# A mixture-of-experts loop with the picking matmuls ahead of the scatter group and other PSUM banks for scatter and gather

## The chip, the core and the metric

The kernel runs on one core of one Trainium2 chip. The metric is device time of one execution in microseconds (us), lower is better. The core's engines run side by side, each with a queue of its own that it works off strictly in order: TensorE (PE; its weight loads are shown as PEld), VectorE (DVE), ScalarE (ACT), GpSimd (POOL), and SyncE (SP), which here issues the DMAs. A matmul writes to PSUM, which this kernel uses as eight tiles of 128 partitions x 512 float32 values; such a tile is called a bank below. DVE and ACT read a bank, and only then may a later matmul overwrite it.

## What is computed

One decoder layer on 512 tokens of width 1024: an attention part, then a hierarchical mixture of experts with 32 experts and two chosen per token. The change lies wholly in the second part, which is, cut to its core:

```python
for e in range(N_EXPERTS):
    h = jax.nn.silu(t @ w_gate[e]) * (t @ w_up[e])
    y = y + combine[:, e:e + 1] * (h @ w_down[e]).astype(jnp.float32)
```

Here `combine` holds the gates of the two chosen experts of each token and zero elsewhere. A 1024 x 512 gate matrix, a 1024 x 512 up matrix and a 512 x 1024 down matrix belong to each expert, all float32.

## The kernel before

The kernel does not run every expert over every token. It handles the 32 experts as 16 pairs (`NP = 16`, counted by `q`). For each pair it gathers up to 64 tokens of each expert into 128 rows, computes with these rows alone, and adds the result back to the residual `hx` (512 x 1024, held in SBUF). Gathering and adding back are matmuls with one-hot matrices. The steps of one pair:

- `pick_a` (L766) and `pick_h` build the one-hot matrix `ohh` (DVE) and a bfloat16 copy `ohb` (ACT).
- `pick_g` (L803) is twelve very small matmuls (L809, 4 columns each) that pick the gate, the token number and the norm factor of each gathered row into bank `pm`. Two small DVE copies (L811, L812) move them to `idf`.
- `x_rows` (L834), called twice, gathers the rows of the normed input: 32 matmuls of 128 x 128 in each call (L839), then one DVE multiply (L843) that empties the bank into `xT`. The first call (`g` = 0) uses bank `pm`, the second bank `po`.
- `mm_in` (L941) is the gate product (`u` = 0) and the up product (`u` = 1); the second ends with a DVE multiply into `sg` (L958). `h_t` (L962) transposes that result through a bank `pt`, and `mm_down` (L971) is the down product, in two halves of 512 columns. `ev_down` (L987) moves each half to SBUF as a pair `yh`, `yl`.
- `comb` (L1084) adds one half to the residual for one block of 128 tokens `i`: two matmuls (L1092, L1093) into a bank, then one DVE addition to `hx` (L1094). `combs` (L1145) calls it for `i` = 0, 1, 2, 3; this is the scatter group. The banks are `pm`, `po`, `pt`, `pt` in this order.
- `over_prep` (L996), once, at pair 1, counts the tokens that do not fit into 64 rows: four matmuls (L999) into `po`, four DVE instructions that read it (L1001, L1003), then a chain on POOL. `over_loop` at the end of the program treats those tokens; in the profiled execution it made no round.

The order is written out by hand in the loop at L1149 and no scheduler changes it. In iteration `q` the products of pair `q` run, and the rows of pair `q + 1` are gathered. After the up product of pair `q` the order is: the scatter group for the second half of pair `q - 1`, (`over_prep` if `q` = 1), `pick_g(q + 1)`, `x_rows(q + 1, 0)`, `h_t(q)`, `x_rows(q + 1, 1)`, the down product and the scatter group for the first half of pair `q`.

Bank names stand for pools: there is one `pm`, one `po`, two `pt`, two `pjt` (down product) and two `ps_s` (gate and up product). Weights come by DMA into a ring of 21 units of 1 MB (plus one spare); `load` (L619) issues the next unit when the matmuls that read the old content have been passed, in the order gate, up, down of each pair. The down weights of the last two pairs come last, in smaller pieces (L631). At the end `finish` (L1098) runs the down product of these two pairs in column pieces (L1105), adds and stores.

Of the kernel before, what the change touches and what calls it, by code (L numbers as in the profile page):

```python
# [10 lines left out]
F32 = mybir.dt.float32  # L11
# [28 lines left out]
    g=[5, 10, 7, 12, 6, 1, 1],  # L40
# [544 lines left out]
def moe(ctx, tc, A, out, G):  # L585
    nc = tc.nc
    v, act, pool, pe = nc.vector, nc.scalar, nc.gpsimd, nc.tensor
    hx, ident, mhalf, bcast, spool, pt_tile, warm, colv, colx, rb = (
        G[k] for k in ("hx", "ident", "mhalf", "bcast", "spool", "pt_tile", "warm", "colv", "colx", "rb"))
    pj, psS, psT, psO, psM, split_wo, OPS = (G[k] for k in ("pj", "psS", "psT", "psO", "psM", "split_wo", "OPS"))  # L590
    out = out[0]
    NS = 21
    NP = 16
# [20 lines left out]
    def rows(q, u, e, k):  # L614
        if u == 2:
            return place(AT[q, u], k)[:, e]
        return place(AT[q, u], k // 2)[:, e, 512 * (k % 2):512 * (k % 2) + 512]

    def load(half=None):  # L619
        m, c = divmod(state["n"], 4)  # L620
        state["n"] += half != 0
        if m < 3 * NP - 2:
            d, w = place(m, c), src(m, c)
            if half is not None:
                d, w = (x[:, :, 512 * half:512 * half + 512] for x in (d, w))
            nc.sync.dma_start(d, w)
        elif m < 3 * NP and c == 3:
            cut = CUT[MO[m][0]]
            for lo, hi in zip(cut, cut[1:]):
                for k in range(4):  # L630
                    nc.sync.dma_start(place(m, k)[:, :, lo:hi], src(m, k)[:, :, lo:hi])  # L631
# [62 lines left out]
    def tmp(n, *shape, dt=F32, tag=None):  # L694
        return me.tile([128] + list(shape), dt, name=n, tag=tag or n)
# [77 lines left out]
    def pick_h(q):  # L773
        OHB[q] = me.tile([128, 4, 128], BF16, name="ohb")
        if q:
            act.activation(OHB[q], OHH[q], AF.Copy)
        else:
            act.activation(OHB[q][:, :2], OHH[q][:, :2], AF.Copy)
            act.activation(OHB[q][:, 2:], OHN[q][:, 2:], AF.Copy)
# [7 lines left out]
    def half(i, c):  # L787
        return H[i // 2][:, c, i % 2]
# [14 lines left out]
    def pick_g(q):  # L803
        p = psM.tile([128, 512], F32, name="pm")
        for i in range(4):
            for j in range(3):
                c = g3[:, j, i, 0:1]
                c = bass.AP(tensor=c.tensor, offset=c.offset, ap=[list(c.ap[0]), [2 + 2 * q, 2], [1, 2]])
                pe.matmul(p[:, 0:4], OHB[q][:, i, :], c, start=(i == 0 and j == 0), stop=(i == 3 and j == 2))  # L809
        ID[q] = me.tile([128, 3], F32, name="idf", bufs=3)  # L810
        v.tensor_copy(ID[q], p[:, 0:3])  # L811
        v.tensor_copy(ID[q][64:128, 2:3], p[64:128, 3:4])  # L812
# [19 lines left out]
                v.tensor_scalar(x, t, g, None, op0=OP.mult)  # L832

    def x_rows(q, g):  # L834
        p = (psO.tile([128, 4, 128], F32, name="po") if g else psM.tile([128, 4, 128], F32, name="pm"))
        for k in range(4):
            for i in range(4):
                for c in range(2):
                    pe.matmul(p[:, k, :], half(i, c)[:, 4 * g + k, :], OHH[q][:, i, :],  # L839
                              start=(i == 0 and c == 0), stop=(i == 3 and c == 1))  # L840
        if g == 0:
            XT[q] = G["m2_"].tile([128, 8, 128], F32, name="xT")
        v.tensor_mul(XT[q][:, 4 * g:4 * g + 4, :], p, colg[:, 4 * g:4 * g + 4].unsqueeze(2).to_broadcast([128, 4, 128]))  # L843
# [97 lines left out]
    def mm_in(q, u, fill=()):  # L941
        p = psS.tile([128, 512], F32, name="ps_s")
        for k in range(8):
            for e in range(2):
                pe.matmul(p[64 * e:64 * e + 64, :], XT[q][:, k, 64 * e:64 * e + 64], rows(q, u, e, k),  # L945
                          start=(k == 0), stop=(k == 7))
            if q == 0 and 8 * u + k < PRM["qk"]:
                if k // 2 != 2 or u:
                    load(k % 2)
            elif k % 2 and (q or u or k != 5):  # L950
                load()
            for j in range(k * len(fill) // 8, (k + 1) * len(fill) // 8):
                fill[j]()
        if u == 0:
            GT[q] = me.tile([128, 512], F32, name="sg")
            act.activation(GT[q], p, AF.Silu, scale=1.0 if q else ID[q][:, 0:1])
        elif q:
            v.tensor_mul(GT[q], GT[q], p)  # L958
        else:
            v.scalar_tensor_tensor(GT[q], p, ID[q][:, 0:1], GT[q], op0=OP.mult, op1=OP.mult)  # L960

    def h_t(q):  # L962
        t = pt_tile()
        for k in range(4):
            pe.transpose(t[:, k, :], GT[q].rearrange("p (c k) -> p k c", k=4)[:, k], ident)  # L965
        HT[q] = me.tile([128, 4, 128], F32, name="hTt", tag="ohn" if q == NP - 2 else "sg")
        act.activation(HT[q], t, AF.Copy)  # L967
# [16 lines left out]
    def y_pair(q):  # L984
        return [me.tile([128, 512], F32R, name=f"y{c}", tag=f"y{c}") for c in "hl"]

    def ev_down(q, n):  # L987
        yh, yl = YH[q, n] = y_pair(q)
        p = DN.pop((q, n))
        g = ID[q][:, 2:3]  # L990
        act.activation(yh, p, AF.Copy, scale=g)  # L991
        v.scalar_tensor_tensor(yl, p, g, yh, op0=OP.mult, op1=OP.subtract)  # L992
# [3 lines left out]
    def over_prep():  # L996
        p = psO.tile([128, 512], F32, name="po")
        for i in range(4):
            pe.matmul(p[:, :32], one, mb[:, i, :], start=(i == 0), stop=(i == 3))  # L999
        te, ca, cb = tmp("te", 32), tmp("ca", 32), tmp("cb", 32)  # L1000
        v.tensor_scalar(te, p[:, :32], 64.0, None, op0=OP.is_gt)  # L1001
        for j in range(1, 4):
            v.scalar_tensor_tensor(te, p[:, :32], 64.0 + 128.0 * j, te, op0=OP.is_gt, op1=OP.add)  # L1003
        cur, nxt = te, ca
        for d in (1, 2, 4, 8, 16):
            pool.tensor_copy(nxt[:, :d], cur[:, :d])
            pool.tensor_add(nxt[:, d:], cur[:, d:], cur[:, :32 - d])
            cur, nxt = nxt, (cb if nxt is ca else ca)
        pool.tensor_sub(te, cur, te)
        c2 = me.tile([128, 4, 32], F32, name="c2", tag="L")  # L1010
        pool.tensor_scalar(nxt, te, 128.0, -64.0, op0=OP.mult, op1=OP.add)
        pool.tensor_add(c2, code, nxt.unsqueeze(1).to_broadcast([128, 4, 32]))
        nt = me.tile([128, 1], I32, name="nt")
        pool.tensor_copy(nt, cur[:, 31:32])
        gi = tmp("gi", 1)
        pool.memset(gi, 0.0)
        OV.update(lo=te, hi=cur, scr=nxt, c2=c2, gi=gi, nt=nt)
# [66 lines left out]
    def comb(q, n, i, store=False):  # L1084
        yh, yl = YH[q, n]
        ns = slice(512 * n, 512 * n + 512)
        if i < 2 or store:
            p = psO.tile([128, 512], F32, name="po") if i % 2 else psM.tile([128, 512], F32, name="pm")
        else:
            p = pt_tile().rearrange("p a b -> p (a b)")  # L1090
        oh = OH[q][:, 128 * i:128 * i + 128]
        pe.matmul(p, oh, yh, start=True, stop=False)  # L1092
        pe.matmul(p, oh, yl, start=False, stop=True)  # L1093
        v.tensor_add(hx[:, i, ns], hx[:, i, ns], p)  # L1094
        if store:
            nc.sync.dma_start(out[128 * i:128 * i + 128, ns], hx[:, i, ns])
# [48 lines left out]
    def combs(q, n):  # L1145
        for i in range(4):
            comb(q, n, i)

    for q in range(NP):  # L1149
        fill = []  # L1150
        if q == 0:
            fill = [lambda: None, lambda: pick_g(0), lambda: pick_h(1)]
        elif q == 1:
            fill = [lambda: None, lambda: combs(0, 0), lambda: ev_down(0, 1)]
        if q < NP - 1:
            pick_a(q + 1)
            if q:
                pick_h(q + 1)
        mm_in(q, 0, fill)
        if q == 0:  # L1160
            split_h(2)
            split_h(3)
        mm_in(q, 1)
        if 0 < q < NP - 1:
            combs(q - 1, 1)
        if q == 1:
            over_prep()
        if q < NP - 1:
            pick_g(q + 1)
            x_rows(q + 1, 0)  # L1170
        h_t(q)
        if q < NP - 1:
            x_rows(q + 1, 1)
        oh_s(q)
        if q == 0:
            mm_down(q, (0, 1))
            ev_down(q, 0)
        elif q < NP - 2:
            mm_down(q, (0,))
            ev_down(q, 0)  # L1180
            mm_down(q, (1,))
            combs(q, 0)
            ev_down(q, 1)
    finish()
    over_loop()

# [59 lines left out]
```

## Time and profile before

| what | value |
|---|---|
| time, median of 3 runs | 800.59 us (799.62 to 801.36) |
| the profiled execution: its own time | 800.3 us |
| its span, first to last instruction | 798.5 us |
| mean granted TensorE clock | 0.994 of full speed |
| PE busy | 760.6 us, 95% of the span |
| DVE busy | 386.5 us, 48% |
| ACT busy | 198.0 us, 25% |
| POOL busy | 121.8 us, 15% |

The profile is one execution. Its times count from the first instruction; the time of the execution is 1.8 us longer than the span. A row of the trace names source line, engine, operation, the tile written and the tiles read, and in brackets for how long the engine had been idle before it and what ended that. Idle time of an engine off the path that ends last costs nothing.

### The profile page before, as it was taken

The numbers are of one execution on the slowest core, as the hardware profiler recorded it, in microseconds if no ns is written. First come the engines' busy times: TensorE is split into PE (matmuls) and PEld (weight loads), VectorE is DVE, ScalarE is ACT, GpSimd is POOL, SyncE is SP. The second block draws the span as 40 slices with busy tenths as digits, with TensorE's granted clock in tenths as the row PEclk, the third lists the DMA queues.
The fourth block names the chain that finished last, engine by engine and source line by source line (L and its number), as shares of the span: only waits on it lengthen the run. The fifth ranks groups of instructions, "written<-read, shape, count | busy, mean of one in ns | idle before, by whom it ended". The sixth has DMA issues, their size and how long they took to land.

```text
span 798.5 us, 12313 instructions
## 1 busy us (share of the span) xinstructions
PE 760.6 (95%) x4848; PEld 473.0 (59%) x4848; DVE 386.5 (48%) x924; ACT 198.0 (25%) x426; POOL 121.8 (15%) x213
## 2 busy tenths in 40 slices
PE   8989999999999999999999999999999999999996
PEld 8868877888967884344443443443543543544455
DVE  5787887777877364333333322422522423333234
ACT  6534445444552434100100100101101001001011
POOL 2767551432312120010000000000000000000000
PEclk9999999999999999999999999999999999999999
DMA  8522022244576888999999999999999999999603
GB/s 327 174 80 70 11 87 85 95 139 153 211 275 212 317 309 297 385 345 412 405 409 408 407 408 409 409 408 408 408 409 409 409 409 408 407 409 364 209 1 108
DMA packets 78140, 231.68 MB, mean 290 GB/s; under 512 B 5113, under 2 KB 20857, under 8 KB 78081
## 3 DMA queue, kind: packets, MB, share of 16 engines
q1 hardware_dynamic: 78080, 230.88, 76.1%
q8 instruction: 39, 0.64, 0.3%
q14 instruction: 21, 0.16, 0.1%
HBM read 228.75 MB, written 2.11 MB: 289 GB/s over the span
## 4 chain that ended last, share of the span: by engine, by line
PE 75%; DVE 15%; DMA 3%; ACT 3%; issue 1%; POOL 1%; SPq 1%; DVEq 0%; ACTq 0%
PE ps_s L945 26%; PE pjt L977 12%; DVE hx L1094 4%; PE pm L839 4%; PE po L839 3%; PE pjt L226 3%; DMA wr<-in_wq_dram 3%; PE pjt L228 3%; PE pjt L227 3%; PE po L389 2%; PE pjt L1105 2%; PE pjt L448 2%; PE ps_s L356 2%; PE pjt L449 2%; PE pjt L450 2%; PE pt L382 2%
## 5 line engine op out<-in xcount | busy, mean ns | idle before, releaser
L958 DVE TENSOR_TENSOR sg<-sg,ps_s 128x512 f32<-128x512 f32 x15 | 10.3, 687 | 170.6 <-PE ps_s L945 170.6
L967 ACT ACTIVATE hTt<-pt 128x512 f32<-128x512 f32 x16 | 9.6, 597 | 186.2 <-PE pt L965 186.2
L991 ACT ACTIVATE yh<-pjt,idf 128x512 fp32r<-128x512 f32 x28 | 19.2, 687 | 134.0 <-PE pjt L977 70.3
L364 ACT ACTIVATE z<-z,sm 128x128 f32<-128x128 f32 (+3 forms) x64 | 35.5, 555 | 42.9 <-DVE sm L362 42.7
L251 POOL TENSOR_TENSOR ss<-ss,mhalf 128x4 f32<-128x4 f32 x32 | 34.8, 1088 | 60.2 <-DVE ss L250 55.9
L839 PEld LDWEIGHTS <-ha 128*128 128x128 f16 x480 | 32.0, 98 | 19.2 <-DVE idf L812 19.1
L992 DVE SCALAR_TENSOR_TENSOR yl<-pjt,idf,yh 128x512 fp32r<-128x512 f32 x28 | 20.9, 747 | 42.0 <-ACT yh L991 42.0
L839 PE MATMUL pm<-ohh,ha 128*128 128x128 f16 x240 | 23.3, 220 | 17.7 <-DVE idf L812 17.7
L227 PE MATMUL pjt<-wsa,xh 128*128 128x384 f32 (+1 forms) x112 | 37.9, 339 | 0.2 <-DVE wsa L149 0.2
L1094 DVE TENSOR_TENSOR hx<-hx,pm 128x512 f32<-128x512 f32 x28 | 19.1, 683 | 37.8 <-PE pm L1093 37.8
L1094 DVE TENSOR_TENSOR hx<-hx,pt 128x512 f32<-128x512 f32 x56 | 35.7, 679 | 0.0
L839 PEld LDWEIGHTS <-hb 128*128 128x128 f16 x480 | 31.8, 98 | 0.0
L226 PE MATMUL pjt<-wsa,xh 128*128 128x384 f32 (+1 forms) x80 | 29.2, 365 | 0.8 <-ACT wsa L148 0.8
L383 DVE COPY PT<-pt 128x128 f32<-128x128 f32 (+3 forms) x64 | 28.2, 481 | 1.8 <-PE pt L382 1.5
L945 PE MATMUL ps_s<-slotr,xT 128*64 128x512 f32 x128 | 28.9, 594 | 0.0
L356 PE MATMUL ps_s<-qks 64*128 64x128 f32 (+3 forms) x192 | 25.5, 356 | 3.4 <-DVE sm L362 2.0
L228 PE MATMUL pjt<-wsa,xl 128*128 128x384 f32 (+1 forms) x80 | 27.1, 339 | 0.0
L227 PE MATMUL pjt<-wsu,xh 128*128 128x384 f32 (+1 forms) x76 | 25.8, 340 | 0.5 <-DVE wsu L149 0.5
L382 PE MATMUL pt<-ident,z 128*128 128x128 f32 x160 | 23.5, 277 | 3.0 <-DVE PT L383 1.7
L226 PE MATMUL pjt<-wsu,xh 128*128 128x384 f32 (+1 forms) x72 | 26.3, 365 | 0.0
L945 PE MATMUL ps_s<-slotxh,xT 128*64 128x512 f32 x112 | 25.4, 595 | 0.0
L945 PE MATMUL ps_s<-slot,xT 128*64 128x512 f32 x112 | 25.3, 594 | 0.0
(426 smaller groups left out, 1737.3 us busy)
## 6 DMA issues: line engine op xcount, KB each, us to landing
wr<-in_wq_dram SPq DMA_DIRECT2D x28, 384.0 KB, 3.9
slotr<-in_w_up_dram SPq DMA_DIRECT2D x8, 1024.0 KB, 8.0
slotr<-in_w_gate_dram SPq DMA_DIRECT2D x8, 1024.0 KB, 13.1
slot<-in_w_gate_dram SPq DMA_DIRECT2D x8, 1024.0 KB, 13.5
slotwr<-in_w_up_dram SPq DMA_DIRECT2D x8, 1024.0 KB, 15.8
slotr<-in_w_down_dram SPq DMA_DIRECT2D x8, 1024.0 KB, 11.7
slotxh<-in_w_up_dram SPq DMA_DIRECT2D x7, 1024.0 KB, 10.2
slotmhl<-in_w_gate_dram SPq DMA_DIRECT2D x7, 1024.0 KB, 14.4
```

Of the source, the lines that this page charges most:

```text
L226: pe.matmul(ps[:, :n], xh[:, k, t], wh, start=(k == 0), stop=False)
L227: pe.matmul(ps[:, :n], xh[:, k, t], wl, start=False, stop=False)
L228: pe.matmul(ps[:, :n], xl[:, k, t], wh, start=False, stop=(k == 7))
L251: pool.tensor_tensor(ss[:, 4:8], ss[:, 0:4], mhalf[:, 0:4], op=OP.pow)
L356: pe.matmul(pss[h][:, :n], q[d, t], k[d, :n], start=(k is kh and q is qh), stop=(q is ql))
L364: act.activation(z[:, :n], z[:, :n], AF.Exp, bias=nm, scale=-1.0, accum_out=l)
L382: pe.transpose(t[:, j, :], z[:, 128 * j:128 * j + 128], ident)
L383: v.tensor_copy(PT[p][h][:, :i + 1, 128 * i:128 * i + 128], t[:, :i + 1, :])
L839: pe.matmul(p[:, k, :], half(i, c)[:, 4 * g + k, :], OHH[q][:, i, :], start=(i == 0 and c == 0), stop=(i == 3 and c == 1))
L945: pe.matmul(p[64 * e:64 * e + 64, :], XT[q][:, k, 64 * e:64 * e + 64], rows(q, u, e, k), start=(k == 0), stop=(k == 7))
L977: pe.matmul(DN[q, n][64 * e:64 * e + 64, :], HT[q][:, k, 64 * e:64 * e + 64], rows(q, 2, e, k)[:, 512 * n:512 * n + 512], start=(k == 0), ...
L1094: v.tensor_add(hx[:, i, ns], hx[:, i, ns], p)
```

## The change

Three things change, and no arithmetic does. First, in the loop at L1149 `pick_g(q + 1)` is called right after the up product, ahead of the scatter group. Second, `over_prep` of pair 1 moves from there to the end of that iteration. Third, banks are handed out in another order: `x_rows` uses `po` for its first call and `pm` for its second, and the scatter group uses `po`, `pt`, `pt`, `pm`. (`comb` with `store`, which `over_loop` alone uses, alternates between `po` and `pm` as before, with the two swapped.)

```diff
     def x_rows(q, g):
-        p = (psO.tile([128, 4, 128], F32, name="po") if g else psM.tile([128, 4, 128], F32, name="pm"))
+        p = (psM.tile([128, 4, 128], F32, name="pm") if g else psO.tile([128, 4, 128], F32, name="po"))
...
     def comb(q, n, i, store=False):
-        if i < 2 or store:
-            p = psO.tile([128, 512], F32, name="po") if i % 2 else psM.tile([128, 512], F32, name="pm")
+        if i in (1, 2) and not store:
+            p = pt_tile().rearrange("p a b -> p (a b)")
         else:
-            p = pt_tile().rearrange("p a b -> p (a b)")
+            p = psO.tile([128, 512], F32, name="po") if i in (0, 2) else psM.tile([128, 512], F32, name="pm")
...
         mm_in(q, 1)
+        if q < NP - 1:
+            pick_g(q + 1)
         if 0 < q < NP - 1:
             combs(q - 1, 1)
-        if q == 1:
-            over_prep()
         if q < NP - 1:
-            pick_g(q + 1)
             x_rows(q + 1, 0)
...
             ev_down(q, 1)
+            if q == 1:
+                over_prep()
```

On TensorE, behind an up product in the middle of the loop, the kernel before has (`yh` and `yl` are the evicted down product, `ohs` the one-hot matrix that scatters, `g` and `ohb` the operands of the picking, `ha` a part of the normed input):

```order
L945 MATMUL ps_s<-slotqkb,xT 64x512 x4
L1092 MATMUL pm<-yh,ohs 128x512
L1093 MATMUL pm<-yl,ohs 128x512
L1092 MATMUL po<-yh,ohs 128x512
L1093 MATMUL po<-yl,ohs 128x512
...
L809 LDWEIGHTS ohb
L809 MATMUL pm<-g_2976,ohb 128x4
...
L839 LDWEIGHTS ha
L839 MATMUL pm<-ohh,ha 128x128
```

and the changed kernel:

```order
L945 MATMUL ps_s<-slotqkb,xT 64x512 x4
L809 LDWEIGHTS ohb
L809 MATMUL pm<-g_2976,ohb 128x4
...
L1092 MATMUL po<-yh,ohs 128x512
L1093 MATMUL po<-yl,ohs 128x512
...
L1092 MATMUL pm<-yh,ohs 128x512
L1093 MATMUL pm<-yl,ohs 128x512
L839 LDWEIGHTS ha
L839 MATMUL po<-ohh,ha 128x128
```

The picking moved ahead of the eight scatter matmuls, the last scatter bank is now the one that the picking wrote, and the gather's first bank is the one that the scatter group wrote first.

On VectorE the same place reads before:

```order
L958 TENSOR_TENSOR sg<-sg,ps_s 128x512
L1094 TENSOR_TENSOR hx<-hx,pm 128x512
L1094 TENSOR_TENSOR hx<-hx,po 128x512
L1094 TENSOR_TENSOR hx<-hx,pt 128x512 x2
L811 COPY idf<-pm 128x3
L812 COPY idf<-pm 64x1
L843 TENSOR_TENSOR xT<-pm,colg 128x512
L843 TENSOR_TENSOR xT<-po,colg 128x512
```

and after the change:

```order
L958 TENSOR_TENSOR sg<-sg,ps_s 128x512
L811 COPY idf<-pm 128x3
L812 COPY idf<-pm 64x1
L1094 TENSOR_TENSOR hx<-hx,po 128x512
L1094 TENSOR_TENSOR hx<-hx,pt 128x512 x2
L1094 TENSOR_TENSOR hx<-hx,pm 128x512
L843 TENSOR_TENSOR xT<-po,colg 128x512
L843 TENSOR_TENSOR xT<-pm,colg 128x512
```

The two small copies moved ahead of the four additions to `hx`. On ACT, POOL and SP the order of the instructions is the same in both kernels.

## Rows read from the trace of the kernel before

**Rows 1.** The page: busy time of each engine, then the chain of work that ended last, by engine, as shares of the span.

```profile
PE 760.6 (95%) x4848; PEld 473.0 (59%) x4848; DVE 386.5 (48%) x924; ACT 198.0 (25%) x426; POOL 121.8 (15%) x213
...
PE 75%; DVE 15%; DMA 3%; ACT 3%; issue 1%; POOL 1%; SPq 1%; DVEq 0%; ACTq 0%
```

**Rows 2.** Busy time of each engine in chosen stretches: two iterations, each from one first gather to the next. Columns: stretch, length, then busy us (instructions) of PE, PEld, DVE, ACT, POOL, then granted clock, busy share of the 16 DMA engines, GB/s.

```profile
470.33:501.10 30.77, 29.61 (x192) 14.03 (x192) 10.01 (x18) 3.20 (x5) 0.00 (x0) 1.00 1.03 409
501.10:531.87 30.77, 29.60 (x193) 14.03 (x193) 10.02 (x18) 3.20 (x5) 0.00 (x0) 1.00 1.03 408
```

**Rows 3.** The chain of work that ended last in order of time, from a scatter group (pair 7) to the gather behind the next up product (start us, us, what).

```profile
514.47 13.91 PE ps_s L945 x64
...
528.47 0.69 DVE sg L958
529.15 2.39 DVE hx L1094 x4
531.54 0.08 DVE idf L811
...
531.65 0.17 DVE idf L812
...
531.87 1.96 PE pm L839 x32
533.83 0.53 PE pt L965 x4
```

**Rows 4.** The same place in the instructions in order of time, TensorE alone (start us, us, engine, line, operation, tiles, shapes, count, idle time before and what ended it).

```profile
530.02 0.39 PE L1093 MATMUL pt<-yl,ohs 128*128 128x512 f32 x1
530.25 0.45 PE L809 MATMUL pm<-g,ohb 128*128 128x4 bf16 x12
531.87 0.40 PE L839 MATMUL pm<-ohh,ha 128*128 128x128 f16 x4 [1.16 <-DVE idf L812]
```

**Rows 5.** The same place, all engines: the first scatter matmul behind the up product, and what VectorE does.

```profile
526.46 1.89 PE L945 MATMUL ps_s<-slotqkb,xT 128*64 128x512 f32 x8
...
528.28 0.50 PE L1092 MATMUL pm<-yh,ohs 128*128 128x512 f32 x1
...
528.47 0.69 DVE L958 TENSOR_TENSOR sg<-sg,ps_s 128x512 f32<-128x512 f32 x1 [11.62 <-PE ps_s L945]
...
529.07 0.68 DVE L1094 TENSOR_TENSOR hx<-hx,pm 128x512 f32<-128x512 f32 x1
...
529.67 0.68 DVE L1094 TENSOR_TENSOR hx<-hx,po 128x512 f32<-128x512 f32 x1
...
530.27 1.27 DVE L1094 TENSOR_TENSOR hx<-hx,pt 128x512 f32<-128x512 f32 x2
531.46 0.15 DVE L811 COPY idf<-pm 128x3 f32<-128x3 f32 x1
531.65 0.16 DVE L812 COPY idf<-pm 64x1 f32<-64x1 f32 x1
```

**Rows 6.** Who waited for whom on TensorE and on its weight loads from 300 us to the end (us in total, times, longest us); of the rows that name a DMA, the largest.

```profile
PE pm L839 <- DVE idf L812: 17.7, 15, 1.7
PE pt L965 <- DVE sg L958: 0.9, 1, 0.9
...
PEld L839 <- DVE idf L812: 19.1, 15, 1.8
...
PEld ps_s L945 <- DMA slotmhl<-in_w_up_dram: 1.1, 4, 0.3
```

**Rows 7.** Instructions in order of time where the first picking (pair 0) stands between matmuls of a gate product, TensorE and then VectorE.

```profile
305.26 0.45 PE L809 MATMUL pm<-g,ohb 128*128 128x4 bf16 x12
305.64 1.08 PE L945 MATMUL ps_s<-slotxh,xT 128*64 128x512 f32 x4
...
305.75 0.16 DVE L811 COPY idf<-pm 128x3 f32<-128x3 f32 x1 [0.48 <-PE pm L809]
```

**Rows 8.** Instructions in order of time at the end of the up product of pair 0, and of pair 1, where `over_prep` stands.

```profile
310.51 4.14 DVE L798 SCALAR_TENSOR_TENSOR hb<-hx,rbig,hb 128x1024 f16<-128x1024 f32 x2 [4.40 <-ACT hb L796]
...
314.38 0.45 PE L809 MATMUL pm<-g,ohb 128*128 128x4 bf16 x12
314.68 0.75 DVE L960 SCALAR_TENSOR_TENSOR sg<-ps_s,idf,sg 128x512 f32<-128x512 f32 x1
...
315.75 0.40 PE L839 MATMUL pm<-ohh,ha 128*128 128x128 f16 x4 [0.92 <-DVE idf L812]
...
342.93 0.50 PE L1092 MATMUL pm<-yh,ohs 128*128 128x512 f32 x1
...
344.90 0.29 PEld L999 LDWEIGHTS <-one 128*128 128x128 bf16 x4 [0.28 <-issue]
...
345.13 0.37 PEld L809 LDWEIGHTS <-ohb 128*128 128x128 bf16 x12
...
347.29 0.40 PE L839 MATMUL pm<-ohh,ha 128*128 128x128 f16 x4 [1.70 <-DVE idf L812]
```

**Rows 9.** One weight unit through the ring: its issue on SP's queue, the matmuls that read it (with the count), and how long all DMAs of L626 took from issue to landing.

```profile
511.59 0.37 SPq L626 DMA_DIRECT2D slotmhl0b<-in_w_up_dram  x1
...
557.22 1.89 PE L945 MATMUL ps_s<-slotmhl0b,xT 128*64 128x512 f32 x8
...
DMA to landing us min/median/max: 4.7/11.5/17.7
```

**Rows 10.** The end of the weight traffic, in stretches with the columns of rows 2, and the last down products in the instructions in order of time.

```profile
720.00:740.00 20.00, 20.00 (x101) 7.68 (x100) 6.01 (x10) 2.60 (x4) 0.00 (x0) 1.00 1.04 361
...
750.00:760.00 10.00, 10.00 (x67) 4.24 (x66) 1.52 (x3) 0.93 (x2) 0.00 (x0) 1.00 0.14 37
760.00:770.00 10.00, 9.14 (x60) 4.22 (x58) 2.00 (x4) 1.07 (x2) 0.00 (x0) 1.00 0.01 2
...
789.42 0.61 PE L1105 MATMUL pjt<-slotx,hTt 128*64 128x128 f32 x8
```

## The prediction

> **What bounds the kernel now.** I read the page first. TensorE is busy for 95% of the span and holds three quarters of the chain that ended last; VectorE holds 15% of it, although it is busy for only 48% of the time [rows 1]. So there are places where TensorE stands still for a VectorE that has little to do. The stretches show where: one iteration of the loop takes 30.77 us, of which TensorE is busy for 29.6, so 1.16 us are missing in each [rows 2]. The chain in order of time shows what fills the hole: it leaves TensorE at the end of the up product, runs through `sg`, four additions to `hx` and the two `idf` copies on VectorE, and comes back to TensorE at the gather [rows 3]. The instructions give the reason. TensorE issues scatter group and picking without a break until 530.7 and then idles until 531.87, when the second copy is done [rows 4]. The gather wants bank `pm`; the picking wrote it; the copies that empty it stand behind the four additions in VectorE's queue [rows 5]. The list of waits has the sum: 15 such waits, 17.7 us on the matmuls, 19.1 us on their weight loads; beside them TensorE waits for an engine in the loop nowhere worth naming [rows 6].
>
> **A steady iteration (q = 2 to 14, thirteen of them).** From the first scatter matmul to the gather it is 528.28 to 531.87, 3.59 us [rows 4, 5]. The work inside: the scatter group takes 530.25 - 528.28 = 1.97 us, and the picking, where it stands between other matmuls with no wait behind it, takes 305.64 - 305.26 = 0.38 us [rows 4, 5, 7]. If nothing waits any more, the gather comes 2.35 us behind the up product, and 3.59 - 2.35 = 1.24 us are saved. The trace's own idle time, 1.16 us, is the lower reading, since it counts the modelled end of the picking (0.45 us) as work [rows 4].
>
> Does nothing wait? I put the new order onto the clock of this iteration. Picking on TensorE from 528.28 to 528.73; a copy has followed the picking within 0.05 us where VectorE was free (305.71 to 305.75) [rows 7], so it is ready before VectorE is. VectorE starts `sg` at 528.47 and its next instruction 0.60 later; the copies then start at 529.07 and 529.26 and end at 529.42 (0.19 apart, 0.16 long) [rows 5]. The additions follow 0.60 apart, 0.68 long: `po` done at 530.1, the two `pt` at 530.7 and 531.3, `pm` at 531.9. Against that TensorE asks:
> - the last scatter pair wants `pm`, which the copies must have left (529.42), at about 528.28 + 0.38 + three quarters of 1.97 = 530.1. Spare: 0.7 us.
> - the first gather wants `po` (530.1) at 528.28 + 2.35 = 530.63. Spare: 0.5 us, the smallest.
> - the transpose wants the first `pt` (530.7) at 530.63 + 1.96 = 532.6 (the gather's length) [rows 3]. Spare: 1.9 us.
> - the second gather wants `pm` (531.9) 0.53 us later, at 533.1. Spare: 1.2 us.
>
> So the wait goes and no other takes its place. The cover is the scatter group: 1.97 us of TensorE work under which VectorE now does the 0.35 us of copies and the first addition. Without it the gather would wait for the copies as at pair 0. The picking's own inputs are ready: `ohb` is made at the beginning of the iteration. The scatter group of the first half has no gather behind it, but the next gate product, which writes other banks, so its new bank order costs nothing.
>
> **Pair 1.** Here the hole is 347.29 - 342.93 = 4.36 us, because the four `over_prep` instructions on VectorE stand ahead of the copies too. Less 1.97, 0.38 and the 0.23 us of `over_prep`'s matmuls (344.90 to 345.13) it is 1.78 us; the trace's idle time is 1.70 [rows 8]. The 0.23 us come back at the end of the iteration, so they cancel. There the matmuls need `po` emptied by the first addition of the group just issued, while three more scatter pairs run; they do not wait. Its four VectorE instructions and the POOL chain then stand beside a 13.9 us stretch of products [rows 3], and nothing needs them before the end of the kernel. Nothing is moved past a DMA on SP or POOL.
>
> **Pair 0.** There is no scatter group, and the order stays, but the first gather now goes to `po` and no longer waits for the copies out of `pm`. The hole is 315.75 - 314.38 - 0.38 = 0.99 us, idle 0.92 [rows 8]. The gather also needs `hb`, which VectorE finishes at 310.51 + 4.14 = 314.65, before it would ask; the transpose behind it needs `sg` (315.43), 1.2 us before its turn.
>
> **Sum.** High reading: 13 x 1.24 + 1.78 + 0.99 = 18.9 us. Low reading: the idle time of the matmuls, 17.7 us; the idle time of the weight loads, 19.1 us, bounds it from above [rows 6]. I take 18.5, nearer to the high reading, because the picking's 0.38 us in a running stream is the row most like the new order.
>
> **Can the weights follow?** This is the cover of the whole sum. In the loop the 16 DMA engines are busy all the time (share 1.03) at 408 GB/s, and 408 x 30.77 us is the 12.55 MB that one pair needs [rows 2]: TensorE and the transfers run at the same pace by now, and a TensorE that needs 29.5 us asks for 425 GB/s, which these rows do not show. It lives on stock then. One unit was issued at 511.59, was there at most 17.7 us later, and was read at 557.22 [rows 9]: at least 27.9 us in advance. The loop gets ahead by 18.5 us in all, so at least 9.4 us are left. At the end nearly all transfers are done by 760, and the last down products run at 789.42 [rows 10], 770.9 after the change. That holds too.
>
> **Rival 1: the wait comes back in part.** The spare of 0.5 us on `po` is small, and I worked it out, I did not see it. If the gather is in fact let go only by the third addition (531.3), 0.57 us are left of each 1.24, 10.2 us with pairs 0 and 1: 790.1 us. By the fourth there is nothing left but pairs 0 and 1. For it: all waits of TensorE on VectorE stand in one queue. Against it: the present gather started within 0.1 us of the copy that it needed [rows 4, 5].
>
> **Rival 2: the transfers are the bound.** If the stock were not there, an iteration would stay at 30.77 us, since the transfers are full; only pairs 0 and 1 and the last two holes, when the large transfers are ending, would gain: 0.99 + 1.78 + 2 x 1.24 = 5.3 us, 795.0 us. Against it stand the 27.9 us, and that the longest wait of a weight load for a DMA in the loop's largest such row is 0.3 us [rows 6, 9]. The Trainium skill, Perfetto Trace Analysis, section Roofline, gives a single core a practical ceiling near 120% of 358 GB/s, which its 16 DMA engines bound at about 435 GB/s in aggregate; by that rule this loop is memory-bound and shorter TensorE work buys nothing. The trace agrees that the transfers are full, and shows them full at 408; what the rule leaves out is the stock in the ring, on which a loop of sixteen rounds can draw.
>
> **Rival 3: slower.** TensorE frees units earlier, so more transfers are queued at once. If that lowered their rate to the 361 GB/s that the small pieces of 720 to 740 us reach [rows 10], a pair's weights would take 34.8 us, 4.0 more; over twelve pairs 48 us less the 27.9 in stock is 20 us late: 820 us. It becomes slower than before where the rate falls under about 380 GB/s (2.3 us a pair). Against it: the engines are full already, with several transfers queued, and hold 408 to 409 [rows 2].
>
> That the change does not do what it says is excluded by the order of the instructions: the picking stands ahead, and the banks are swapped.
>
> **Numbers.** The profiled execution took 800.3 us, 0.3 below the median of 800.59; 800.59 - 18.5 = 782.1. Chances: forecast 0.84, rival 1 0.08, rival 2 0.06, rival 3 0.02. The forecast's own range is 781 to 783.5 (readings of 17.7 to 19.1, and runs that differ by up to 1 us from their median). To hold 8 in 10 with something of rival 1 I give 780.3 to 785.5. A measurement here can tell about 0.2%, 1.6 us, from no change. Faster by more 0.95 (forecast, rivals 1 and 2, less their worst corners), the same 0.02, slower 0.03.
>
> **What would show it.** Right: iterations of about 29.5 us; no wait of the gather for `idf`; copies directly behind `sg`; the last scatter pair and both gathers with no idle time ahead. Wrong: idle time at the gather that names an addition to `hx` (rival 1); weight loads that wait for DMAs by more than 0.4 us late in the loop (rival 2); GB/s in the loop under 400 (rival 3). A granted clock other than 1.00 in the loop would be something that I have not seen coming.

## The result, and the profile after

The changed kernel takes 779.75 us (median of 4 runs, 778.72 to 780.25), the kernel before on the same chip 800.73 us (4 runs, 799.62 to 801.36). The ratio is 0.974, 95% interval 0.972 to 0.976: faster by 20.98 us. The forecast was 782.1 us with a range of 780.3 to 785.5. The sign and the mechanism were right; the gain was 2.5 us larger than forecast, and the time lies 0.55 us below the range. The profiled execution took 779.89 us; its span is 778.0 us.

The page of the changed kernel: busy time of each engine, then the chain that ended last, by engine.

```profile
PE 759.7 (98%) x4848; PEld 473.9 (61%) x4848; DVE 388.1 (50%) x924; ACT 198.0 (25%) x426; POOL 122.8 (16%) x213
...
PE 82%; DVE 9%; DMA 3%; ACT 3%; issue 1%; POOL 1%; SPq 1%; DVEq 0%; ACTq 0%
```

TensorE does the same 760 us of work as in [rows 1], in a shorter span. Its share of the chain rose from 75 to 82%, and VectorE's fell from 15 to 9%: the part of the chain that ran through VectorE in each iteration is gone.

Two iterations of the changed kernel, from first gather to first gather, in the columns of [rows 2]:

```profile
461.65:491.09 29.44, 29.44 (x195) 13.96 (x194) 10.10 (x20) 3.20 (x5) 0.00 (x0) 1.00 1.03 409
491.09:520.53 29.44, 29.44 (x195) 13.96 (x194) 10.10 (x20) 3.20 (x5) 0.00 (x0) 1.00 1.03 408
```

Length and busy time of TensorE are now the same number; 30.77 against 29.61 was the hole. The granted clock is 1.00 and the transfers stand at 408 to 409 GB/s in both kernels.

The chain of the changed kernel in order of time at a scatter group, where [rows 3] left TensorE for 3.4 us:

```profile
504.29 13.88 PE ps_s L945 x64
518.18 0.39 PE pm L809 x12
518.56 0.33 PE po L1092
...
520.30 0.23 PE pm L1093
520.53 1.80 PE po L839 x32
```

It stays on TensorE. The instructions of the changed kernel there in order of time, all engines, beside [rows 4, 5]:

```profile
518.11 0.45 PE L809 MATMUL pm<-g,ohb 128*128 128x4 bf16 x12
518.29 0.69 DVE L958 TENSOR_TENSOR sg<-sg,ps_s 128x512 f32<-128x512 f32 x1 [11.62 <-PE ps_s L945]
518.42 0.47 PE L1092 MATMUL po<-yh,ohs 128*128 128x512 f32 x1
...
518.90 0.15 DVE L811 COPY idf<-pm 128x3 f32<-128x3 f32 x1
519.09 0.16 DVE L812 COPY idf<-pm 64x1 f32<-64x1 f32 x1
519.28 0.69 DVE L1094 TENSOR_TENSOR hx<-hx,po 128x512 f32<-128x512 f32 x1
519.88 1.28 DVE L1094 TENSOR_TENSOR hx<-hx,pt 128x512 f32<-128x512 f32 x2
519.90 0.40 PE L1092 MATMUL pm<-yh,ohs 128*128 128x512 f32 x1
...
520.37 0.40 PE L839 MATMUL po<-ohh,ha 128*128 128x128 f16 x4
...
521.08 0.68 DVE L1094 TENSOR_TENSOR hx<-hx,pm 128x512 f32<-128x512 f32 x1
```

The copies stand right behind `sg`. The last scatter pair writes `pm` 0.65 us after they have left it (519.25 to 519.90), and the gather starts in `po` 0.4 us after the first addition has emptied it (519.97 to 520.37). Neither has idle time ahead. From the start of the picking to the gather it is 2.26 us; the forecast had 2.35.

Every wait of TensorE for another engine from 295 us to the end of the changed kernel (us in total, times, longest us); nothing stands in the place of the first line of [rows 6]:

```profile
PE pt L965 <- DVE sg L958: 0.9, 1, 0.9
PE pm L1134 <- DVE hx L1139: 0.2, 1, 0.2
```

### The profile page after: what moved, and what is told of

Read it like the earlier page. It is cut to its first block, busy times and chain, and to the rows that moved or that the text cites. A ratio compares the mean times of both kernels' runs of the same rounds, so it can differ in the third digit from the quotient of the medians.

```text
span 778.0 us, 12313 instructions
## 1 busy us (share of the span) xinstructions
PE 759.7 (98%) x4848; PEld 473.9 (61%) x4848; DVE 388.1 (50%) x924; ACT 198.0 (25%) x426; POOL 122.8 (16%) x213
## 3 DMA queue, kind: packets, MB, share of 16 engines
HBM read 228.75 MB, written 2.11 MB: 297 GB/s over the span
## 4 chain that ended last, share of the span: by engine, by line
PE 82%; DVE 9%; DMA 3%; ACT 3%; issue 1%; POOL 1%; SPq 1%; DVEq 0%; ACTq 0%
PE ps_s L945 29%; PE pjt L977 13%; PE po L839 3%; PE pm L839 3%; PE pjt L226 3%; PE po L389 3%; PE pjt L228 2%; PE pjt L227 2%; PE pjt L1105 2%; PE pjt L448 2%; PE pt L1093 2%; PE pt L1092 2%; PE ps_s L356 2%; PE pjt L450 2%; PE pjt L449 2%; PE po L1092 1%
## 5 line engine op out<-in xcount | busy, mean ns | idle before, releaser
L1094 DVE TENSOR_TENSOR hx<-hx,po 128x512 f32<-128x512 f32 x28 | 19.3, 688 | 38.3 <-PE po L1093 37.8
L228 PE MATMUL pjt<-wsu,xl 128*128 128x384 f32 (+1 forms) x72 | 24.6, 342 | 0.0
```

Of the source, the lines that this page charges most:

```text
L228: pe.matmul(ps[:, :n], xl[:, k, t], wh, start=False, stop=(k == 7))
```

## The experiments

The change holds three things: other banks, an earlier picking and a later `over_prep`. The first four experiments take them apart, the next two price what the forecast had priced from single rows, and the last two look at the end of the kernel and at chance. Times are medians of the runs, each beside runs of the kernel before on the same chip; the medians of the kernel before differ by 0.5 us among those chips (800.66 to 801.19 us), so that smaller differences between experiments are read from the traces.

**The gather's banks alone**, in the kernel before:

```diff
-        p = (psO.tile([128, 4, 128], F32, name="po") if g else psM.tile([128, 4, 128], F32, name="pm"))
+        p = (psM.tile([128, 4, 128], F32, name="pm") if g else psO.tile([128, 4, 128], F32, name="po"))
```

> Kernel before with one line changed: the first gather call takes bank po, the second pm; picking, scatter order and over_prep stay. Theory (only the bank that the gather shared with the copies made the wait): the gather then waits for the second addition alone, which ends at about 530.4 on the clock of the kernel before, ahead of the 530.6 at which TensorE is there; each of the 13 steady iterations gains the full 1.3 us, pair 0 gains 1.1, pair 1 only about 0.3, since over_prep's reading of po stands in the way. Sum 18.6 us: about 782. Rival (the picking must stand ahead of the scatter group for the gain): the gather waits as before for what stands in VectorE's queue and the time stays within 2 us of 800.7.

Measured: 781.79 us, ratio 0.976 (0.974 to 0.978), against 0.974 for the whole change. One line brings nine tenths of the gain. An iteration of this kernel in stretches, then one picking and gather in the instructions, and the wait of TensorE that is left:

```profile
434.42:463.87 29.45, 29.45 (x198) 13.97 (x196) 10.02 (x19) 3.20 (x5) 0.00 (x0) 1.00 1.03 408
```

```profile
434.12 0.45 PE L809 MATMUL pm<-g,ohb 128*128 128x4 bf16 x12
...
434.43 0.38 PE L839 MATMUL po<-ohh,ha 128*128 128x128 f16 x4
```

```profile
PE po L839 <- DVE te L1003: 1.4, 1, 1.4
```

The picking still stands behind the scatter group and the copies still stand behind four additions, but the gather no longer asks for the bank that they empty, and follows the picking by 0.31 us. So taking the gather off `pm` is enough to close the hole in a steady iteration; the order need not change. What is left is pair 1, where the gather now shares `po` with `over_prep`.

**The order alone**: the changed kernel with the old banks for scatter and gather.

```diff
+        if q < NP - 1:
+            pick_g(q + 1)
         if 0 < q < NP - 1:
             combs(q - 1, 1)
-        if q == 1:
-            over_prep()
         if q < NP - 1:
-            pick_g(q + 1)
             x_rows(q + 1, 0)
```

(and `over_prep` at the end of iteration 1, as in the change)

> Changed kernel with the old banks (scatter group pm, po, pt, pt; gather pm, then po): the picking and over_prep are moved, nothing else. Theory: the first scatter pair wants pm, which the picking wrote and the copies empty only behind sg, so TensorE waits about 0.9 us there in place of 1.3 at the gather; 0.4 us gained in each of 13 iterations, 1.1 at pair 1, nothing at pair 0: about 794. Rival (the move alone brings the gain): about 781.

Measured: 793.81 us, ratio 0.991 (0.990 to 0.993), 30.41 us an iteration. Waits of TensorE and one of the places in the instructions:

```profile
PE pm L1092 <- DVE idf L812: 11.7, 14, 0.8
```

```profile
526.16 0.47 PE L1092 MATMUL pm<-yh,ohs 128*128 128x512 f32 x1 [0.83 <-DVE idf L812]
```

The wait moved to the first scatter matmul, which wants `pm` right behind the picking, while the copies must first let `sg` pass. It is 0.83 us where it was 1.16, and in a steady iteration only the difference is gained (30.76 to 30.41).

**The banks alone**: both bank orders of the change in the kernel before, with picking and `over_prep` at their old places.

> Kernel before with both new bank orders (scatter group po, pt, pt, pm; gather po, then pm) and the old place of picking and over_prep. Theory: the picking now wants pm, which the fourth addition empties last, at about 531.5 on the clock of the kernel before, so the wait moves from the gather to the picking and nearly all of it stays; only pair 0 gains 1.1: 799 to 800. Rival (banks alone bring the gain): about 781.

Measured: 798.68 us, ratio 0.997 (0.996 to 0.998), 30.78 us an iteration. Waits of TensorE, then the place in the instructions:

```profile
PE pm L809 <- DVE hx L1094: 16.5, 14, 1.2
```

```profile
498.82 0.44 PE L809 MATMUL pm<-g,ohb 128*128 128x4 bf16 x12 [1.19 <-DVE hx L1094]
...
499.12 0.38 PE L839 MATMUL po<-ohh,ha 128*128 128x128 f16 x4
```

Here the picking waits, since the scatter group wrote `pm` last. In the pair of profiled executions the gain comes from pair 0 (1.06 us), pair 1 (0.28) and a loop that was reached 0.75 us earlier, which is chance (see the last experiment); a steady iteration gains nothing. So the new scatter banks need the new place of the picking, and the new place needs the new banks; the gather's swap needs neither.

**The gather's banks, and `over_prep` moved**: the one line of the first experiment, and

```diff
-        if q == 1:
-            over_prep()
         if q < NP - 1:
             pick_g(q + 1)
...
             ev_down(q, 1)
+            if q == 1:
+                over_prep()
```

> Kernel before with the first gather in po, the second in pm, and over_prep moved to the end of iteration 1; picking and scatter banks as before. Theory (these two edits are all of the gain): no wait of TensorE on the copies or on over_prep is left, 779 to 780.5, the same as the changed kernel. Rival (the picking ahead of the scatter group adds something of its own): at least 1.5 us above it.

Measured: 779.92 us, ratio 0.974 (0.972 to 0.975): the whole change without the picking's move and without new scatter banks. One iteration of this kernel, in the columns of [rows 2]:

```profile
461.72:491.17 29.45, 29.45 (x199) 13.96 (x195) 10.02 (x19) 3.20 (x5) 0.00 (x0) 1.00 1.03 409
```

In the steady loop (29.45 us here, 29.44 with the whole change) and in the sum the other two edits add nothing that can be measured once the gather has its own bank. What they do change is the spare: the gather finds `po` emptied 0.22 us before it starts in this kernel, and 0.40 us in the changed one.

**The picking twice** in the changed kernel, to price it by itself:

```diff
-        for i in range(4):
+        for i in [x for _ in range(2) for x in range(4)]:
```

> Changed kernel with the twelve picking matmuls issued twice into the same bank, the second round overwriting the first with the same values. It measures what the picking costs in the stream. Theory (start to start, 25 ns a matmul, 0.30 us for twelve): 16 pickings, 4.8 us more than the changed kernel, about 784.6. Rival 1 (0.38 us, the price that the prediction took): 6.1 us more, 785.9. Rival 2 (the busy row, 0.45 us): 7.2 us more, 787.

Measured: 784.49 us, ratio 0.980 (0.978 to 0.981). It is 4.74 us slower than the changed kernel; over 16 pickings that is 0.30 us each (0.27 if each time is taken against the kernel before beside it). The iterations show it without that doubt. Two successive pairs of rows from this kernel's chain in order of time:

```profile
490.55 0.69 PE pm L809 x24
...
493.20 1.80 PE po L839 x32
...
520.29 0.69 PE pm L809 x24
...
522.94 1.80 PE po L839 x32
```

An iteration takes 29.74 us (493.20 to 522.94), 0.30 more than without the second picking.

**Half a gather** in the changed kernel, to draw on the stock of weights harder than the change does:

```diff
-                for c in range(2):
+                for c in range(1):
                     pe.matmul(p[:, k, :], half(i, c)[:, 4 * g + k, :], OHH[q][:, i, :],
-                              start=(i == 0 and c == 0), stop=(i == 3 and c == 1))
+                              start=(i == 0), stop=(i == 3))
```

> Changed kernel whose gather takes the high float16 halves of the normed input alone and leaves the low halves out, so half of the gather's matmuls: 15 gathers of 64 go to 32 each, 1.8 us less TensorE work in each iteration, 27 us in all. It asks how far the loop can get ahead of the weights. In the changed kernel the tightest weight unit is there 17.5 us before its use. Theory (stock): the loop gains until that is spent and then runs at the pace of the transfers, 30.8 us an iteration; 760 to 763, with weight loads waiting for DMAs late in the loop. Rival (transfers speed up when they are asked for more): 753, GB/s over 430 in the loop.

Measured: 762.26 us, ratio 0.952 (0.950 to 0.953). TensorE's work shrinks by some 27 us (15 gathers, 1.8 us each), the time by 17.5. An early iteration and the last two in stretches, each from one first gather to the next, and the largest waits of weight loads for DMAs in the up product:

```profile
398.17:425.83 27.66, 27.66 (x162) 12.18 (x161) 10.02 (x19) 3.20 (x5) 0.00 (x0) 1.00 1.03 409
...
647.05:676.95 29.90, 28.55 (x162) 11.82 (x161) 10.01 (x19) 3.20 (x5) 0.00 (x0) 1.00 1.03 409
676.95:708.96 32.01, 28.76 (x161) 11.71 (x161) 10.02 (x19) 3.20 (x5) 0.00 (x0) 1.00 1.03 408
```

```profile
PEld ps_s L945 <- DMA slotwr<-in_w_up_dram: 3.6, 4, 1.5
PEld ps_s L945 <- DMA slotmhl0a<-in_w_up_dram: 3.1, 2, 1.6
```

As long as there is stock, an iteration takes what TensorE needs, 27.66 us. Once it is spent, in the last two, TensorE idles and they take 29.90 and 32.01 us, 30.96 on average: near the 30.77 us of the kernel before, in which 408 to 409 GB/s deliver one pair's weights. The rate did not rise when more was asked for.

**A down product ahead of the last transpose**: in the changed kernel the first product of `finish` (`down`, of pair 14) goes in front of `h_t(15)`.

```diff
-        y = ev(*seg[0], down(*seg[0]))
+        y = ev(*seg[0], DN["first"])
...
+        if q == NP - 1:
+            DN["first"] = down(NP - 2, *CUT[NP - 2][:2])
         h_t(q)
```

> Changed kernel with the first down product of the last part (pair 14, columns 0 to 255) issued ahead of the transpose of pair 15, which waits 0.9 us for sg. Theory: the wait goes under 1.8 us of matmuls, 0.9 us saved, 778.9. Rival (the weights of that piece or the bank come too late there): no gain or a loss of up to 1 us.

Measured: 778.72 us (777.83 to 779.03), ratio 0.972 (0.971 to 0.974). First the place in the changed kernel, then in this one, TensorE in order of time:

```profile
742.73 1.89 PE L945 MATMUL ps_s<-slotmhl0a,xT 128*64 128x512 f32 x8
...
745.48 0.75 PE L965 MATMUL pt<-ident,sg 128*128 128x128 f32 x4 [0.86 <-DVE sg L958]
```

```profile
742.53 1.89 PE L945 MATMUL ps_s<-slotmhl0a,xT 128*64 128x512 f32 x8
...
744.25 1.47 PE L1102 MATMUL pjt<-slotr,hTt 128*64 128x256 f32 x12
...
746.08 0.75 PE L965 MATMUL pt<-ident,sg 128*128 128x128 f32 x4
```

The last wait of the loop for VectorE is covered by work that was needed anyway. The medians differ by 1.03 us and the wait was 0.86; the runs of the two kernels overlap by 0.3 us, so that the size of this gain is not certain from the times; in the two profiled executions TensorE's work behind the last first gather ends 0.92 us sooner (44.26 against 45.18 us). It is the fastest version found.

**The kernel before, once more**, for a second profile of unchanged code.

> The kernel before once more, for a second profile. Theory: the 0.5 us by which the changed kernel reached the loop earlier are chance of the single execution (transfers at the start), so this profile's first gather lies anywhere within about 0.5 us of 315.75, and its steady iteration is 30.76 us again. Rival: they belong to the change, then this one lies at 315.75 within 0.1 us.

Measured: 801.9 us, one run. Its first gather lies at 315.60 us, 0.15 before the 315.75 of the first profile, and its steady iteration is 30.76 us. That is within the theory's 0.5 us and hardly outside the rival's 0.1, so it decides little by itself. The other profiles say more: kernels with the same code ahead of the loop reach it up to 1.2 us apart (299.16 to 300.37 us over the profiled executions), which bounds what one pair of profiles can say of parts that were not changed.

## Where the forecast was right, and where it missed

**What bounds the kernel, and where the time goes: right.** The hole was the gather's wait for the copies out of `pm`. The first experiment shows it alone: with another bank for the gather and nothing else, the iteration falls from 30.76 to 29.45 us.

**Does nothing wait: right, but for one reason given.** The timetable put the copies at 0.60 us behind `sg`, and they came 0.61 behind; its four spares were positive, and the two that the rows above show were 0.65 and 0.40 us where 0.7 and 0.5 were worked out. Rival 1 did not come about. The second and third experiments show what a wait that only moves looks like: 11.7 us at the scatter, 16.5 us at the picking. (The times of the rivals were counted from the profiled execution, 800.3 us, that of the forecast from the median, 800.59; beside it the rivals' times are 0.3 us low, which decides nothing.) Wrong was that the scatter group is the cover without which the gather would wait for the copies. A gather in `po` does not wait for them at all: with the bank of the gather alone changed they stand behind the four additions as before, and the gather follows the picking by 0.31 us.

**A steady iteration: mis-sized, and this is the step that failed.** It said 1.24 us, and the iteration became 1.32 us shorter (30.76 to 29.44). The 3.59 us from first scatter matmul to gather became 2.26 instead of 2.35. The term that was wrong is the price of the picking, 0.38 us from [rows 7]. Between the picking and the scatter it is 0.31 (518.11 to 518.42 above), and the picking doubled cost 0.30 each. The row of the 0.38 does not hold for the new place: between the gate products the changed kernel still takes 0.38 (304.75 to 305.13), and with the picking doubled 0.69:

```profile
304.46 0.75 PE L809 MATMUL pm<-g,ohb 128*128 128x4 bf16 x24
305.15 1.08 PE L945 MATMUL ps_s<-slotxh,xT 128*64 128x512 f32 x4
```

So twelve matmuls cost 0.31 there too, and the other 0.07 belong to that place, where a gate product follows, and not to the picking; why it costs them is not shown. The rest, 0.02, is the scatter group, 1.95 instead of 1.97. Over thirteen iterations that is 1.1 us.

**The idle time as a bound: wrong, in the step on the sum.** The forecast took the matmuls' idle time, 17.7 us, for the low reading and that of the weight loads, 19.1 us, for a bound from above. The loop gained more than either. The first matmul of the gather behind pair 0, 1 and 14's up products moved from 315.75, 347.29 and 747.20 us to 314.19, 343.62 and 726.45; the first gate product from 299.95 to 299.45. So pair 0 gained 1.06 us (0.99 said), pair 1's gather 2.11 (2.01 by the forecast's terms, of which 0.23 were to be paid back, so 1.78; about 0.11 was paid back in the next iteration, 29.55 us in place of 29.44), and the rest 17.08: together 20.25 us, against 18.9 by the high reading. The reason lies in how idle time is counted: it starts at the modelled end of the last picking matmul, 0.45 us after the first one's start, but the next matmul can start 0.31 after it. Each hole was thus about 0.14 us longer than its idle time, and 1.16 + 0.14 gives 1.30 of the 1.32. Start to start it comes out directly: 530.25 to 531.87 in [rows 4] is 1.62 us, less 0.31 is 1.31. The Trainium skill, Perfetto Trace Analysis, section Tensor Engine Instruction (MATMUL, LD_WEIGHTS), says that the profiler estimates a matmul's end and does not observe it; the 0.45 beside 0.31 agrees.

**The missing 2.48 us in all.** Of these, 1.36 are the loop (1.07 from the steady iterations, 0.23 from pair 1, 0.07 from pair 0, rounded). Another 0.39 is that 18.5 was taken although the sum gave 18.9. The start of the loop and the end behind the last gather give 0.16 (0.50 less 0.34), which lies within what unchanged code scatters. The last 0.57 lies between the one pair of profiled executions (20.41 us) and the medians. The range was too narrow by the wrong bound: with the loop's real 20.25 us the forecast would have been 780.3, and runs that lie up to 1 us from their median then belong in the range.

**Pair 1 and `over_prep`: right in kind.** With the gather in `po`, the iteration that holds it takes 31.27 us where `over_prep` stands ahead of the gather and 29.45 where it stands at the end (from pair 0's first gather to pair 1's, first and fourth experiments), 1.82 less; of that 0.24 come back in the next iteration, and 0.11 in the changed kernel.

**Can the weights follow: right.** One late unit in the changed kernel: its issue on SP's queue, the matmuls that read it, and how long all DMAs of L626 took from issue to landing.

```profile
706.25 1.78 SPq L626 DMA_DIRECT2D slotmhl0a<-in_w_up_dram  x1
...
742.73 1.89 PE L945 MATMUL ps_s<-slotmhl0a,xT 128*64 128x512 f32 x8
...
DMA to landing us min/median/max: 3.7/17.0/19.7
```

It was there at least 16.8 us before it was read (36.5 less 19.7), more than the 9.4 that were counted on; by its own landing, 19.0 us, it was 17.5. Rival 2 did not come about with this change, and the half gather shows where it does: its time fell by 17.5 us more and no further, although TensorE had 27 us less to do. By the rule of the Trainium skill, Perfetto Trace Analysis, section Roofline, that the forecast quoted, this loop is bound by its transfers. The trace agrees that they are full, at 408 to 409 GB/s in every full stretch, below the 435 that the page gives; the 2.6% were gained all the same, out of stock. Rival 3 did not come about: the rate stayed at 408 to 409.

## What to carry to other kernels

When an engine waits for a bank, look first at who shares the bank and at what stands in the queue of the engine that empties it: here another bank for one operation brought nine tenths of the gain, moving `over_prep` nearly all of the rest, and moving the picking nothing more. Price a hole from start to start of the instructions around it, and a short matmul by the distance to its follower; the idle time that is left after modelled ends is too small a number, and no bound. Where the transfers already run full, ask how many us of stock lie between landing and use, since that, and not the rate alone, decides what a shorter compute loop brings.

## What the runs showed of the hardware

**Transfers queue longer at the same rate.** With TensorE ahead, units come free sooner. The rate did not change, 408 to 409 GB/s, but the median from issue to landing rose from 11.5 us [rows 9] to 17.0; at the same rate that means that more transfers are under way at once. Issues on SP's queue that took 0.37 us, as in [rows 9], became longer: the longest at L626 took 3.97 us in the changed kernel and 1.53 in the kernel before. Two of the changed kernel:

```profile
501.41 0.48 SPq L626 DMA_DIRECT2D slotmhl0b<-in_w_up_dram  x1
502.27 2.89 SPq L626 DMA_DIRECT2D slotr7a<-in_w_down_dram  x1
```

**A dip of the clock behind a hole.** In the second profile of the kernel before, TensorE stood at the end of the 1.7-us hole at pair 1 when the granted clock fell. Three iterations in stretches, in the columns of [rows 2], then two slices of 1 us in the second of them:

```profile
315.60:347.14 31.54, 29.84 (x196) 14.20 (x197) 10.68 (x22) 3.20 (x5) 0.26 (x2) 1.00 1.02 393
347.14:379.44 32.30, 31.14 (x192) 15.55 (x193) 10.01 (x18) 3.20 (x5) 2.71 (x14) 0.95 0.91 353
379.44:410.20 30.76, 29.60 (x192) 14.03 (x192) 10.01 (x18) 3.20 (x5) 0.00 (x0) 1.00 1.03 407
```

```profile
347.00:348.00 1.00, 0.86 (x9) 0.86 (x10) 0.09 (x1) 0.00 (x0) 0.87 (x6) 0.50 1.04 418
...
350.00:351.00 1.00, 1.00 (x11) 0.99 (x10) 0.33 (x1) 0.00 (x0) 0.35 (x3) 0.80 1.03 414
```

The granted clock was 0.50, the level of 1.2 GHz, from 347 us on, 0.80 in the slice from 350, and 1.00, the level of 2.4 GHz, from 351; the mean over the iteration is 0.95, and its neighbours had 1.00. The iteration took 32.30 us, 1.55 more than the same one in the first profile (30.75 us, from 347.29 to 378.04). The first profile had the same hole and no such dip, so it does not follow from the hole each time, and whether the hole caused it was not tried.
